# Attention outputs of the neighbourhood heads stored by block, tables loaded a block earlier, and result rows in five buffers that are first read six steps behind their load

## The chip, the cores and the metric

The kernel runs on one core of a Trainium2 chip. The metric is the device time of one execution in microseconds (us). Names of engines are those of the profile: PE (TensorE matmuls), PEld (its weight loads), DVE (VectorE), ACT (ScalarE), POOL (GpSimd), SP (SyncE, which here only issues DMAs; SPq is its queue in the trace).

## The reference

Two layers of a transformer over 2048 latent tokens (a grid of 32 rows by 64 columns) and 256 context tokens, width 1024, all in float32. Cut to what matters here, one layer is:

```
q, k, v, ... = split(h @ w_in)                       # three groups of heads
mix_a = windowed attention with sink, 6 heads        # 384 columns
mix_b = gated short convolution                      # 256 columns
mix_c = neighbourhood attention, 6 heads             # 384 columns
        s = q . k / 8 + rel_pos_bias[dr, dc]         # window of 8 grid rows x 16 columns, and all context keys
x = layer_norm(alpha * x + gate1 * (concat(mix_a, mix_b, mix_c) @ w_out))
route each of 16 experts to its 256 best tokens      # expert choice
acc = alpha * x + sum over experts of gate * swiglu(x[chosen]) at the chosen rows
x = layer_norm(acc)                                  # after layer 1: the output, 2048 x 1024
```

In layer 1 only the latent tokens are computed past the projections.

## The kernel before

Each layer l runs four phases one after another: phase_in (projections), phase_att, phase_out (output projection, first layer norm) and phase_moe (routing is between the two). float32 matmuls are done as three matmuls on a high part (cast by ACT) and a low part (subtracted by DVE). Instructions of an engine and the DMAs of a queue run in the order in which the program emits them. The waits between engines are put in by the framework that the kernel is written with; SP's DMAs share eight completion lanes (DMAHW0 to 7) in rotation, so that each also waits for the one eight before it on its lane.

**Attention.** phase_att works through two A units (the windowed heads) and then six C units, one for each neighbourhood head. A C unit has blocks n = 0 to 3, each a group of 16 grid columns with all 32 rows; in layer 0 a block 4 of context tokens comes first. A block has four steps m of 128 queries; in each, PE makes logits `lg` (L1088, L1089), DVE adds a bias table and takes the maximum (L1113, a custom instruction that also moves the logits), ACT exponentiates (L1121), PE transposes the probabilities (L1139, L1162), ACT and DVE make their high and low parts `ph`, `pl` (L1267, L1258), and PE multiplies with the values (L1197). At a block's end the result is transposed back (L1215), divided by the sums (reciprocal L1226, multiplication L1234) and stored to the DRAM tensor MIXC. A group of blocks shares one tile `o`: reciprocal, multiplication and store come at a group's last block. Groups are the blocks (4), (0, 1), (2, 3), and in the last unit (4), (0, 1), (2), (3). A store is issued in four pieces a block (L1246), by SP, but by POOL for the last block of all.

The bias tables of a unit (`bias` and `va`, 128 x 2048) are made by POOL (bias_part, L1052: three instructions a table) from a tile `toep`, which SP loads in load_unit behind the unit's k (two DMAs of 64 x 2304) and context values vx. load_unit for the next unit is called at block 1 of the present one; before it in each block, more_queries and more_values load q and vw some blocks ahead.

**Output projection.** phase_out loads for each tile of 128 tokens `mix` (384 columns from MIXA, 384 from MIXC), transposes these on PE (L1352), splits them on ACT and DVE (L1354, L1356) and multiplies with w_out (L1369), whose high and low parts are made by ACT and DVE on the way (L178, L186). Ahead of the first tile SP issues the loads of two tiles and of some row vectors (`row`, L1318). The scratch of phase_att and phase_out lie over each other in SBUF, by the order in which the pools are opened.

**Experts and the last layer norm.** phase_moe runs 16 experts. T and F are lists of generators that a tick advances; a tick follows each group of matmuls, 16 an expert. In layer 1, experts 13 to 15 (FINK = 3) run beside the final layer norm of the result's rows: fin_early takes a buffer `fx` (3 of them) or an unused one (`xe`, fin_next), loads 128 rows of ACC (L1841, SP), and adds fin_tile, which waits FINGO = 2 ticks, sums the rows on ACT (L1866), squares them (L1872), scales them on DVE (L1887, L1891) and stores them (L1882). The rows that the last three experts chose are gathered, normalised and scattered once more behind them (L1829, L1850). Expert outputs `y` (DVE, L1765) are added to ACC by POOL's scatters (L1784) from four buffers.

Of the kernel before, what the change touches and what calls it, by code (L numbers as in the profile page):

```python
# [7 lines left out]
F32 = mybir.dt.float32  # L8
# [57 lines left out]
FINLAG = 4  # L66
FINGO = 2
FINSTEP = 4
# [156 lines left out]
def build(ctx, tc, t, out):  # L225
# [47 lines left out]
    def dr(name, shape, dt=F32):  # L273
        return [dram.tile(shape, dt, name=f"{name}{i}") for i in range(DEPTH)]
# [8 lines left out]
    MIXA = dr("MIXA", [TT, 384])  # L283
    MIXC = dr("MIXC", [TT, 384])
    MODR = dr("MODR", [2, 48 * 128])
# [615 lines left out]
    def phase_att(l):  # L901
# [15 lines left out]
        hp.append(pool("at_h1"))  # L917
        lp.append(pool("at_w1"))
        shift(es, 64)
        kp.append(pool("at_k1"))  # L920
        op = pool("at_o", 3)
        bsp = pool("at_bias")
# [16 lines left out]

        units, blks, st = {}, {}, {}  # L940
        blist, mem = [], []
# [10 lines left out]
        for kind, u in [("A", 0), ("A", 1)] + [("C", u) for u in range(6)]:  # L952
            for rows in (range(2, 6), range(6, 10), range(10, 14), range(14, NT), (0, 1)) if kind == "A" else (
                    ((4,), (0, 1), (2,), (3,)) if u == 5 else ((4,), (0, 1), (2, 3))):
                for j, n in enumerate(rows):
                    group[kind, u, n] = ((kind, u, rows[0]), j, len(rows))
# [8 lines left out]
        def load_unit(kind, u):  # L965
# [17 lines left out]
            if kind == "C":  # L983
                v = vxp.tile([128, 2, 128], F32R, name="vx")
                SY.dma_start(v.bitcast(F32), vs[:, 0:2, 2 + u, :])
                r["v"] = v

                tz = tp.tile([128, 16, 64], F32, name="toep")
                rp = t["rpb"][l, u]
                n = 15 * 64 + 48  # L990
                SY.dma_start(tz.rearrange("p i j -> p (i j)")[:, 0:n],
                             bass.AP(tensor=rp.tensor, offset=rp.offset + 15, ap=[[64, 8], [-1, 16], [1, n]]))
                r["toep"] = tz

# [41 lines left out]
        def bias_part(u, ct, rt):  # L1036
# [8 lines left out]
            if rt == 0:  # L1045
                r["bias", ct] = biases[ct % 2 if u % 2 == 0 else 1 - ct % 2]
            b, tz = r["bias", ct], r["toep"]
            j0 = (16, 8, 0)[ct]
# [8 lines left out]
        def qk(i):  # L1057
            b, m, nm = mem[i]
            kind, u, n = b
            if m == 0:  # L1060
# [8 lines left out]
                if at == ustart[kind, u] + (4 if kind == "A" else 1) and x < len(ulist):  # L1069
                    load_unit(*ulist[x])  # L1070
                if (kind, u) == ("C", 5) and at == ustart[kind, u] + 1:
                    W.open(6, 8)
# [94 lines left out]
        def pv(b, nm):  # L1167
# [72 lines left out]
            elif n == 4:  # L1240
                SY.dma_start(MIXC[l][0:256, 64 * u:64 * u + 64].rearrange("(m p) d -> p m d", p=128), all_)
            else:
                dst = MIXC[l][256:TT, 64 * u:64 * u + 64].rearrange("(m a g b) d -> m g a b d", m=4, a=8, g=4)
                for x in range(ng):
                    for m in range(4):
                        (G if b == blist[-1] else SY).dma_start(dst[m, n0 + x], all_[:, 4 * x + m, :])  # L1246
            del st["of", g]
# [55 lines left out]
    def phase_out(l, aff):  # L1303
# [34 lines left out]
        def load_c(n):  # L1338
            SY.dma_start(loaded[n][0][:, 384:768], MIXC[l][tiles[n] * 128:tiles[n] * 128 + 128, :])

# [235 lines left out]
    def phase_moe(l, aff):  # L1576
# [182 lines left out]
        def put(e, n, a, j, py, ys, gates):  # L1759
            yield STEP  # L1760
            if j == 0:
                ys[a] = sb.tile([128, D], F32, name="y", bufs=4)
            y = ys[a][:n, 512 * j:512 * j + 512]
# [41 lines left out]
        def fin_next():  # L1805

            while True:
                for name, n in (("fx", 3), ("xe0", 2), ("xe1", 2)):
                    got = used.setdefault(name, [])
# [50 lines left out]
        def fin_tile(n):  # L1860

            m = fp.tile([128, 6], F32, name="fm", bufs=10)
            sq = junk[:, 0:D]
            for _ in range(FINGO):
                yield STEP
# [212 lines left out]
```

## Time and profile before

| | |
|---|---|
| median of 3 runs | 4123.91 us (4122.41 to 4124.77) |
| the profiled execution | 4118.89 us, its span 4117.1 us |
| busy share of the span | PE 92%, DVE 70%, ACT 49%, POOL 18% |
| mean granted TensorE clock | 0.957 of full speed |
| C units of layer 0 | 808 to 1056 us |
| phase_out of layer 0, first matmul | 1067.80 us |
| C units of layer 1 | 2895 to 3126 us |
| phase_out of layer 1, first matmul | 3136.82 us |
| experts 13 to 15 of layer 1, with the final norm | 3936 to 4067 us |
| what is left behind the last expert | 4067 to 4117 us |

The execution that the profiler recorded took 5.0 us less than the median of the unprofiled runs; the span is that of the trace within it. An engine's busy time is the union of its instructions, so a share below 100% on PE is time in which PE waited.

### The profile page before, as it was taken

What the parts mean: (1) busy time and instruction counts of PE and PEld (TensorE: products, weight loads), DVE (VectorE), ACT (ScalarE), POOL (GpSimd) and SP (SyncE); (2) the same over time, 40 slices, a digit from 0 to 9 for tenths busy, and PEclk for the clock granted to TensorE, in tenths of its full rate; (3) what the DMA queues carried; (4) which work ended last, traced back from release to release, by engine and by line L of the source; (5) the groups of instructions that cost most, each with busy time, mean ns of one, the idle gap of its engine ahead of it and who ended that gap; (6) DMA issues with size and microseconds to landing.
All of it is one profiled execution on the core that took longest, in us unless ns stands there. A gap on an engine that the chain in (4) does not pass through costs nothing. (4 is left out here: it accounts for less than half of the span.)

```text
span 4117.1 us, 63491 instructions
## 1 busy us (share of the span) xinstructions
PE 3801.6 (92%) x23004; PEld 3249.1 (79%) x23004; DVE 2869.1 (70%) x5588; ACT 2010.3 (49%) x3884; POOL 726.0 (18%) x680
## 2 busy tenths in 40 slices
PE   7999999998898899999996999999988976999983
PEld 5887888887787378998984888889887865999972
DVE  6555559987677467777756766479876777777765
ACT  4344339987433144444433534369875333444453
POOL 0000000122133023232211100000321221221214
PEclk9999999999999899999998999999999987999996
DMA  7566674578743677777756765573887424888885
GB/s 238 167 209 192 202 207 129 111 148 154 231 158 126 191 238 227 221 214 209 214 169 218 236 200 183 175 194 88 148 156 209 172 107 156 246 253 257 245 241 185
DMA packets 763969, 784.68 MB, mean 191 GB/s; under 512 B 140224, under 2 KB 645800, under 8 KB 761608
## 3 DMA queue, kind: packets, MB, share of 16 engines
q1 hardware_dynamic: 727800, 656.44, 54.7%
q0 software_dynamic: 34704, 123.13, 10.8%
q8 instruction: 182, 2.98, 0.3%
q10 hardware_dynamic: 1152, 1.05, 0.1%
q14 instruction: 131, 1.07, 0.1%
HBM read 601.98 MB, written 178.48 MB: 190 GB/s over the span
## 5 line engine op out<-in xcount | busy, mean ns | idle before, releaser
L178 ACT CAST wh<-wraw 128x1024 fp32r<-128x1024 f32 x636 | 657.2, 1051 | 394.1 <-DMA wraw<-in_w_in 121.8
L186 DVE TENSOR_TENSOR wl<-wraw,wh 128x1024 fp32r<-128x1024 f32 x636 | 751.5, 1216 | 40.9 <-ACT wh L178 40.7
L1258 DVE TENSOR_TENSOR pl<-pt,ph 128x256 fp32r<-128x256 f32 (+2 forms) x792 | 361.0, 496 | 27.0 <-ACT ph L1267 12.4
L635 PE MATMUL gem<-hh,wh 128*128 128x512 f32 (+1 forms) x960 | 352.9, 368 | 0.0
L1267 ACT CAST ph<-pt 128x256 fp32r<-128x256 f32 (+2 forms) x792 | 310.2, 447 | 86.7 <-PE pt L1139 69.6
L1121 ACT ACTIVATE p<-lg,mx 128x640 f32<-128x640 f32 (+3 forms) x408 | 332.2, 814 | 40.0 <-DVE mx L1113 38.4
L637 PE MATMUL gem<-hh,wl 128*128 128x512 f32 (+1 forms) x960 | 348.6, 363 | 0.0
L636 PE MATMUL gem<-hl,wh 128*128 128x512 f32 (+1 forms) x960 | 347.0, 361 | 0.0
L1922 PE MATMUL pu<-xh,wh 128*128 128x288 f32 (+1 forms) x1024 | 303.1, 296 | 9.2 <-DVE sa L1750 9.2
L1922 PE MATMUL pa<-xh,wh 128*128 128x288 f32 (+1 forms) x1024 | 299.7, 293 | 0.0
L1088 PE MATMUL lg<-k,q 128*128 128x384 f32 (+2 forms) x768 | 282.0, 389 | 17.7 <-ACT p L1121 8.9
L1923 PE MATMUL pa<-xl,wh 128*128 128x288 f32 (+1 forms) x1024 | 295.7, 289 | 0.0
L1924 PE MATMUL pa<-xh,wl 128*128 128x288 f32 (+1 forms) x1024 | 295.7, 289 | 0.0
L1924 PE MATMUL pu<-xh,wl 128*128 128x288 f32 (+1 forms) x1024 | 295.4, 288 | 0.0
L1923 PE MATMUL pu<-xl,wh 128*128 128x288 f32 (+1 forms) x1024 | 295.0, 288 | 0.0
L1642 POOL DMA_INDIRECT xe<-H,ix x80 | 161.1, 2014 | 469.0 <-DVE ix L1637 349.5
L1089 PE MATMUL lg<-k,q 128*128 128x256 f32 x816 | 228.1, 286 | 0.3 <-DVE pl L1258 0.3
L1784 POOL DMA_INDIRECT ACC<-y,ix x62 | 123.3, 1989 | 583.3 <-DVE y L1765 323.2
L1959 PE MATMUL py<-wh,gh 128*128 128x512 f32 x512 | 206.3, 403 | 18.4 <-ACT gh L1752 9.9
L810 PE MATMUL gem<-wh,hh 128*128 128x512 f32 x544 | 219.3, 403 | 1.0 <-ACT hh L603 1.0
L811 PE MATMUL gem<-wl,hh 128*128 128x512 f32 x544 | 215.6, 396 | 1.4 <-DVE wl L186 1.4
L812 PE MATMUL gem<-wh,hl 128*128 128x512 f32 x544 | 215.5, 396 | 0.0
(367 smaller groups left out, 9659.5 us busy)
## 6 DMA issues: line engine op xcount, KB each, us to landing
wraw<-in_w_in SPq DMA_DIRECT2D x160, 512.0 KB
wraw<-in_w_gate SPq DMA_DIRECT2D x128, 512.0 KB
wraw<-in_w_up SPq DMA_DIRECT2D x128, 512.0 KB
wraw<-in_w_down SPq DMA_DIRECT2D x128, 512.0 KB
wraw<-in_w_mod SPq DMA_DIRECT2D x88, 512.0 KB
vw<-VS SPq DMA_DIRECT2D x192, 128.0 KB
q<-QA SPq DMA_DIRECT2D x204, 96.0 KB
VS<-vs SPq DMA_DIRECT2D x36, 512.0 KB
```

Of the source, the lines that this page charges most:

```text
L178: self.nc.scalar.copy(h, self.raw[i])
L186: self.nc.vector.tensor_tensor(e[1], self.raw[i], e[0].bitcast(F32), op=ALU.subtract)
L635: P.matmul(pg[:, t0:nt], wh[:, cs_], hh[:, k, t0:nt], start=(k == 0), stop=False)
L636: P.matmul(pg[:, t0:nt], wh[:, cs_], hl[:, k, t0:nt], start=False, stop=False)
L637: P.matmul(pg[:, t0:nt], wl[:, cs_], hh[:, k, t0:nt], start=False, stop=(k == KD - 1))
L1088: P.matmul(pl[:, w0:512], q[:, x, m, :], win(k), start=(x == 0), stop=(x == 1))
L1121: S.activation(p[:, 0:768 - w0], rec["lg"][:, w0:768], AF.Exp, bias=st[b]["mx"][:, m:m + 1], scale=-1.0, accum_out=st[b]["ss"][:, m:m + 1])
L1258: V.tensor_tensor(view(st[b]["pl"]), src, view(st[b]["ph"].bitcast(F32)), op=ALU.subtract)
L1267: S.copy(view(st[b]["ph"]), src)
L1922: P.matmul(pp[f], wh[:, cs_], xh[:, kk, :], start=(kk == 0), stop=False)
L1923: P.matmul(pp[f], wh[:, cs_], xl[:, kk, :], start=False, stop=False)
L1924: P.matmul(pp[f], wl[:, cs_], xh[:, kk, :], start=False, stop=(kk == KD - 1))
```

## The change

Five things are changed.

1. The rows of the neighbourhood heads lie in a tensor MIXC (context, unchanged form) and a new MIXL [4, 128, 4, 384] (block, partition, m, column), which has the form of the tile `o`: a block's store is one DMA of 128 partitions x 4 x 64 instead of four. Each block is a group of its own, so reciprocal and multiplication come once a block.
2. load_c reads the 128 latent rows of a tile from MIXL by two DMAs of 64 partitions.
3. The pool at_o (tile `o`) is opened ahead of shift() and at_k1, two pools of the same size changing places.
4. `toep` is loaded by a function of its own, in the iteration of the first block of the unit before instead of its second, where k and vx are still loaded.
5. FINGO is 6 (1 once the last expert is through), `fx` has five buffers, and `y` two in the last layer.

```diff
--- before.py
+++ after.py
@@ -64,7 +64,7 @@
 
 FINK = 3
 FINLAG = 4
-FINGO = 2
+FINGO = 6
 FINSTEP = 4
 FINSTEP2 = 2
 
@@ -281,7 +281,9 @@
     VS = dr("VS", [TT, 8, 128])
     OB = dr("OB", [2, 128, 2, TT])
     MIXA = dr("MIXA", [TT, 384])
-    MIXC = dr("MIXC", [TT, 384])
+
+    MIXC = dr("MIXC", [CTX, 384])
+    MIXL = dr("MIXL", [4, 128, 4, 384])
     MODR = dr("MODR", [2, 48 * 128])
     H2 = [dram.tile([n, HX], F32, name=f"H2{n}") for n in (TT, SEQ)]
     ACC = dr("ACC", [SEQ, D])
@@ -916,9 +918,9 @@
         lp = [pool("at_w0")]
         hp.append(pool("at_h1"))
         lp.append(pool("at_w1"))
+        op = pool("at_o", 3)
         shift(es, 64)
         kp.append(pool("at_k1"))
-        op = pool("at_o", 3)
         bsp = pool("at_bias")
         tp = pool("at_toep", 2)
         vwp = pool("at_vw", 3)
@@ -937,7 +939,7 @@
         biases = [None, bsp.tile([128, BWID], F32, name="bias")]
         sink = sinks[:, l, :]
 
-        units, blks, st = {}, {}, {}
+        units, blks, st, toeps = {}, {}, {}, {}
         blist, mem = [], []
         for u in range(2):
             blist += [("A", u, n) for n in range(2, NT)] + ([] if last else [("A", u, 0), ("A", u, 1)])
@@ -951,7 +953,7 @@
         group = {}
         for kind, u in [("A", 0), ("A", 1)] + [("C", u) for u in range(6)]:
             for rows in (range(2, 6), range(6, 10), range(10, 14), range(14, NT), (0, 1)) if kind == "A" else (
-                    ((4,), (0, 1), (2,), (3,)) if u == 5 else ((4,), (0, 1), (2, 3))):
+                    [(n,) for n in range(5)]):
                 for j, n in enumerate(rows):
                     group[kind, u, n] = ((kind, u, rows[0]), j, len(rows))
         ulist = [("A", u) for u in range(2)] + [("C", u) for u in range(6)]
@@ -985,12 +987,14 @@
                 SY.dma_start(v.bitcast(F32), vs[:, 0:2, 2 + u, :])
                 r["v"] = v
 
-                tz = tp.tile([128, 16, 64], F32, name="toep")
-                rp = t["rpb"][l, u]
-                n = 15 * 64 + 48
-                SY.dma_start(tz.rearrange("p i j -> p (i j)")[:, 0:n],
-                             bass.AP(tensor=rp.tensor, offset=rp.offset + 15, ap=[[64, 8], [-1, 16], [1, n]]))
-                r["toep"] = tz
+        def load_toep(u):
+
+            tz = tp.tile([128, 16, 64], F32, name="toep")
+            rp = t["rpb"][l, u]
+            n = 15 * 64 + 48
+            SY.dma_start(tz.rearrange("p i j -> p (i j)")[:, 0:n],
+                         bass.AP(tensor=rp.tensor, offset=rp.offset + 15, ap=[[64, 8], [-1, 16], [1, n]]))
+            toeps[u] = tz
 
         def load_queries(at):
             b = blist[at]
@@ -1044,7 +1048,7 @@
                     G.memset(biases[0][:, o:o + 256], 0.0)
             if rt == 0:
                 r["bias", ct] = biases[ct % 2 if u % 2 == 0 else 1 - ct % 2]
-            b, tz = r["bias", ct], r["toep"]
+            b, tz = r["bias", ct], toeps[u]
             j0 = (16, 8, 0)[ct]
             i0, n = ((4, 12), (0, 16), (0, 12))[rt]
             o = BOFF[rt]
@@ -1068,6 +1072,8 @@
                 more_values(at + 3)
                 if at == ustart[kind, u] + (4 if kind == "A" else 1) and x < len(ulist):
                     load_unit(*ulist[x])
+                if at == ustart[kind, u] and x < len(ulist) and ulist[x][0] == "C":
+                    load_toep(ulist[x][1])
                 if (kind, u) == ("C", 5) and at == ustart[kind, u] + 1:
                     W.open(6, 8)
             k = units[kind, u]["k"]
@@ -1238,12 +1244,9 @@
                 SY.dma_start(MIXA[l][128 * n0:128 * (n0 + ng), 192 * u:192 * u + 192].rearrange("(b p) c -> p b c", p=128),
                              all_.rearrange("p (b m) d -> p b (m d)", b=ng))
             elif n == 4:
-                SY.dma_start(MIXC[l][0:256, 64 * u:64 * u + 64].rearrange("(m p) d -> p m d", p=128), all_)
+                SY.dma_start(MIXC[l][:, 64 * u:64 * u + 64].rearrange("(m p) d -> p m d", p=128), all_)
             else:
-                dst = MIXC[l][256:TT, 64 * u:64 * u + 64].rearrange("(m a g b) d -> m g a b d", m=4, a=8, g=4)
-                for x in range(ng):
-                    for m in range(4):
-                        (G if b == blist[-1] else SY).dma_start(dst[m, n0 + x], all_[:, 4 * x + m, :])
+                (G if b == blist[-1] else SY).dma_start(MIXL[l][n][:, :, 64 * u:64 * u + 64], all_)
             del st["of", g]
 
         gens = []
@@ -1336,7 +1339,13 @@
                 load_c(n)
 
         def load_c(n):
-            SY.dma_start(loaded[n][0][:, 384:768], MIXC[l][tiles[n] * 128:tiles[n] * 128 + 128, :])
+            m, i = loaded[n][0], tiles[n]
+            if i < 2:
+                SY.dma_start(m[:, 384:768], MIXC[l][i * 128:i * 128 + 128, :])
+                return
+            src = MIXL[l].rearrange("g (a b) m c -> m a g b c", b=16)[(i - 2) // 4]
+            for r in range(2):
+                SY.dma_start(m[64 * r:64 * r + 64, 384:768], src[2 * ((i - 2) % 4) + r])
 
         def load_x(n):
             if n >= len(tiles):
@@ -1759,7 +1768,7 @@
         def put(e, n, a, j, py, ys, gates):
             yield STEP
             if j == 0:
-                ys[a] = sb.tile([128, D], F32, name="y", bufs=4)
+                ys[a] = sb.tile([128, D], F32, name="y", bufs=2 if last else 4)
             y = ys[a][:n, 512 * j:512 * j + 512]
             if a < 2:
                 V.scalar_tensor_tensor(y, py, gates[:, a:a + 1], g2[:, 512 * j:512 * j + 512], op0=ALU.mult, op1=ALU.mult)
@@ -1805,7 +1814,7 @@
         def fin_next():
 
             while True:
-                for name, n in (("fx", 3), ("xe0", 2), ("xe1", 2)):
+                for name, n in (("fx", 5), ("xe0", 2), ("xe1", 2)):
                     got = used.setdefault(name, [])
                     q = len(got)
                     if name == "fx":
@@ -1861,7 +1870,8 @@
 
             m = fp.tile([128, 6], F32, name="fm", bufs=10)
             sq = junk[:, 0:D]
-            for _ in range(FINGO):
+
+            for _ in range(1 if "end" in flags else FINGO):
                 yield STEP
             S.activation(sq, xs[n], AF.Copy, accum_out=m[:, 5:6])
             yield STEP
```

On SP's queue in the C units of layer 1, before (the stretch that holds one toep load; q and vw are queries and values, k and vx those of the next unit, MIXC<-o the stores):

```order
1001 L1009 DMA q_26948<-QC_85 64x8x64 x3
1002 L1021 DMA vw<-VS_89 32x8x128 x4
1003 L978 DMA k<-KC_87 64x2304 x2
1004 L985 DMA vx<-VS_89 128x2x128
1005 L991 DMA toep<-in_rpb 128x1x1008
1006 L1009 DMA q_26949<-QC_85 64x8x64 x3
1007 L1021 DMA vw<-VS_89 32x8x128 x4
1008 L1246 DMA MIXC_95<-o 8x16x64 x8
1009 L1009 DMA q_26950<-QC_85 64x8x64 x3
```

The same engine and unit in the changed kernel:

```order
1012 L1025 DMA vw<-VS_89 32x8x128 x4
1013 L995 DMA toep<-in_rpb 128x1x1008
1014 L1249 DMA MIXL_97<-o 512x1x64
1015 L1013 DMA q_26960<-QC_85 64x8x64 x3
1016 L1025 DMA vw<-VS_89 32x8x128 x4
1017 L980 DMA k<-KC_87 64x2304 x2
1018 L987 DMA vx<-VS_89 128x2x128
1019 L1249 DMA MIXL_97<-o 512x1x64
1020 L1013 DMA q_26961<-QC_85 64x8x64 x3
```

toep stands ahead of a block's q and vw and of k and vx, where it stood behind them, and eight stores on two blocks have become two, one a block.

On SP's queue at the end of attention in layer 0 and at the start of phase_out, before, with what each DMA waits for (the four rows ahead of these are stores as well; `m` is a row vector, POOL's DMAs are on lanes DMASW):

```order
803 L1246 DMA MIXC_94<-o 8x16x64 [waits DMAHW0_49,DVE_49]
804 L1246 DMA MIXC_94<-o 8x16x64 [waits DMAHW1_49]
805 L1246 DMA MIXC_94<-o 8x16x64 [waits DMAHW2_49]
806 L1246 DMA MIXC_94<-o 8x16x64 [waits DMAHW3_49]
807 L1329 DMA mix<-MIXA_92 128x384 [waits DMAHW4_49]
808 L1333 DMA mh<-OB_90 128x2x128 [waits DMAHW5_49]
809 L1333 DMA ml<-OB_90 128x2x128 [waits DMAHW6_49]
810 L1329 DMA mix<-MIXA_92 128x384 [waits DMAHW7_49]
811 L1333 DMA mh<-OB_90 128x2x128 [waits DMAHW0_49]
812 L1333 DMA ml<-OB_90 128x2x128 [waits DMAHW1_49]
813 L1318 DMA m_11795<-MODR_96 128x1024 [waits DMAHW2_49,PE_49,Activation_49]
814 L1345 DMA xr<-in_ctx 128x1024 [waits DMAHW3_49,DVE_49]
```

The same place in the changed kernel:

```order
735 L1249 DMA MIXL_96<-o 512x1x64 [waits DMAHW4_49,DVE_49]
736 L1249 DMA MIXL_96<-o 512x1x64 [waits DMAHW5_49,DVE_49]
737 L1249 DMA MIXL_96<-o 512x1x64 [waits DMAHW6_49,DVE_49]
738 L1332 DMA mix<-MIXA_92 128x384 [waits DMAHW7_49]
739 L1336 DMA mh<-OB_90 128x2x128 [waits DMAHW0_49]
740 L1336 DMA ml<-OB_90 128x2x128 [waits DMAHW1_49]
741 L1332 DMA mix<-MIXA_92 128x384 [waits DMAHW2_49]
742 L1336 DMA mh<-OB_90 128x2x128 [waits DMAHW3_49]
743 L1336 DMA ml<-OB_90 128x2x128 [waits DMAHW4_49]
744 L1321 DMA m_11791<-MODR_98 128x1024 [waits DMAHW5_49,DMASW5_49,DMAHW6_49,DVE_49,Activation_49]
745 L1354 DMA xr<-in_ctx 128x1024
```

Three stores stand ahead of the first `mix` load instead of twelve; and the row vector `m` now waits for POOL's store (DMASW5) and for the last of SP's. On ACT, the first cast of w_out in phase_out (the first L178 behind the last L1221) waited for all of POOL's stores and the eight lanes of SP, and waits in the changed kernel for loads of attention, ACT and POOL's instructions, but for no store:

```order
1147 L1221 COPY o_11676<-pt_11670 128x256 [waits DMAHW4_49,DMAHW3_49,DMAHW5_49,DMAHW2_49,DMAHW6_49,DMAHW1_49,DMAHW7_49,DMAHW0_49,PE_49]
1148 L1203 COPY ot_11708<-po_11681 128x512 [waits PE_49]
1149 L1221 COPY o_11715<-pt_11710 128x256 [waits DMAHW7_49,PE_49]
1150 L178 CAST wh_11806<-wraw_11150 128x1024 [waits DMAHW1_49,DMAHW0_49,DMAHW2_49,DMASW7_49,DMAHW3_49,DMASW6_49,DMAHW4_49,DMASW5_49,DMAHW5_49,DMASW0_49,DMAHW6_49,DVE_49,DMAHW7_49,Activation_49,Pool_49]
1151 L178 CAST wh_11809<-wraw_11152 128x1024
1152 L1354 CAST mh_11785<-pt_11815 128x384 [waits PE_49]
1153 L1354 CAST mh_11791<-pt_11820 128x384 [waits PE_49]
```

In the changed kernel:

```order
1147 L1227 COPY o_11678<-pt_11672 128x256 [waits DMAHW3_49,PE_49]
1148 L1209 COPY ot_11707<-po_11683 128x512 [waits PE_49]
1149 L1227 COPY o_11714<-pt_11709 128x256 [waits DMAHW4_49,PE_49]
1150 L178 CAST wh_11802<-wraw_11155 128x1024 [waits DMAHW1_49,DMAHW6_49,DMAHW0_49,DMAHW7_49,Activation_49,Pool_49]
1151 L178 CAST wh_11805<-wraw_11157 128x1024
1152 L1363 CAST mh_11781<-pt_11811 128x384 [waits PE_49]
1153 L1363 CAST mh_11787<-pt_11816 128x384 [waits PE_49]
```

The cast has lost the four lanes DMASW.

On ACT beside expert 13 in layer 1, before, where the first row tile is touched (L178 casts expert weights; L1745 and L1752 belong to an expert's gate):

```order
2694 L178 CAST wh<-wraw 128x1024 x2
2695 L1745 ACTIVATE sa<-pa 128x256 x2
2696 L1866 ACTIVATE junkb,fm<-fx 128x1024
2697 L178 CAST wh<-wraw 128x1024
2698 L1752 CAST gh<-sa 128x256
2699 L1872 ACTIVATE junkb,fm<-fx,fm 128x1024
2700 L1752 CAST gh<-sa 128x256
2701 L1866 ACTIVATE junkb,fm<-fx 128x1024
2702 L1872 ACTIVATE junkb,fm<-fx,fm 128x1024
```

The same place in the changed kernel:

```order
2694 L178 CAST wh<-wraw 128x1024 x2
2695 L1754 ACTIVATE sa<-pa 128x256 x2
2696 L178 CAST wh<-wraw 128x1024
2697 L1761 CAST gh<-sa 128x256 x2
2698 L1876 ACTIVATE junkb,fm<-fx 128x1024
2699 L1882 ACTIVATE junkb,fm<-fx,fm 128x1024
2700 L178 CAST wh<-wraw 128x1024 x2
2701 L1876 ACTIVATE junkb,fm<-fx 128x1024
2702 L178 CAST wh<-wraw 128x1024 x4
```

The first sum over a row tile (L1866, in the changed kernel L1876) comes behind the gate casts L1752 (L1761) of its part of the expert, where it came ahead of them.

## Rows read from the trace of the kernel before

**Rows 1.** Stage windows: length, busy PE, PEld, DVE, ACT, POOL; clock, DMA share, GB/s.

```profile
...
808.00:1056.00 248.00, 227.10 (x1593) 198.72 (x1593) 206.86 (x500) 194.08 (x493) 58.82 (x53) 0.97 0.81 156
2895.00:3126.00 231.00, 213.01 (x1507) 192.25 (x1505) 189.81 (x441) 180.80 (x440) 52.55 (x49) 0.96 0.82 153
3142.00:3385.00 243.00, 228.33 (x1263) 185.75 (x1261) 170.73 (x298) 89.35 (x146) 67.34 (x96) 0.96 0.45 159
3487.00:3917.00 430.00, 428.13 (x3075) 399.96 (x3074) 320.30 (x433) 202.94 (x288) 90.45 (x49) 1.00 0.84 251
3917.00:4067.00 150.00, 117.73 (x759) 106.34 (x758) 100.22 (x147) 74.12 (x118) 32.96 (x36) 0.90 0.75 228
...
```

**Rows 2.** Waits of DVE, C units of layer 1 (us in total, times, longest).

```profile
...
DVE lg L1113 <- POOL bias L1052: 13.4, 4, 6.1
...
DVE lg L1113 <- POOL va L1052: 8.7, 2, 5.0
...
```

**Rows 3.** Timeline of one stall in these units, SP (start us, us, instruction).

```profile
...
2993.26 0.66 SPq L991 DMA_DIRECT2D toep<-in_rpb  x1
...
```

**Rows 4.** Timeline of the same stall, POOL.

```profile
...
3006.11 2.22 POOL L1052 TENSOR_TENSOR bias<-maskC,toep 128x384 f32<-128x384 f32 x2 [30.12 <-DMA toep<-in_rpb]
```

**Rows 5.** Timeline of the same stall, DVE.

```profile
...
2990.56 0.83 DVE L1113 CUSTOM_DVE_ANT_0 lg<-lg,bias 128x640 f32<-128x640 f32 x1 [0.17 <-PE lg L1089]
...
3007.14 0.83 DVE L1113 CUSTOM_DVE_ANT_0 lg<-lg,bias 128x640 f32<-128x640 f32 x1 [6.06 <-POOL bias L1052]
...
```

**Rows 6.** Waits of PE, C units of layer 0.

```profile
...
PE lg L1088 <- DMA q<-QC: 7.2, 4, 3.8
...
```

**Rows 7.** Timeline, end of attention and start of phase_out, layer 0.

```profile
...
1055.13 0.46 SPq L1329 DMA_DIRECT2D mix<-MIXA  x1
...
1057.05 2.49 POOL L1246 DMA_DIRECT2D MIXC<-o  x4 [33.44 <-DVE o L1234]
...
1060.07 0.90 PE L1352 MATMUL pt<-ident,mix 128*128 128x128 f32 x3 [1.42 <-DMA mh<-OB]
...
1065.34 1.99 ACT L178 CAST wh<-wraw 128x1024 fp32r<-128x1024 f32 x2 [9.50 <-DMA xr<-in_ctx]
...
1067.80 0.77 PE L1369 MATMUL po<-wh,mh 128*128 128x512 f32 x1 [6.83 <-ACT mh L1354]
...
```

**Rows 8.** Timeline of the same place in layer 1, all engines.

```profile
...
3125.78 0.37 ACT L1221 COPY o<-pt 128x256 f32<-128x256 f32 x1 [0.75 <-PE pt L1215]
...
3132.01 0.90 PE L1352 MATMUL pt<-ident,mix 128*128 128x128 f32 x3 [1.67 <-DMA mix<-MIXA]
...
3136.82 1.19 PE L1369 MATMUL po<-wh,mh 128*128 128x512 f32 x2 [3.91 <-DMA xr<-X]
...
```

**Rows 9.** Waits of ACT beside the last three experts.

```profile
...
ACT junkb L1866 <- DMA fx<-ACC: 43.1, 8, 9.8
...
```

**Rows 10.** Waits of PE beside the last three experts.

```profile
...
PE py L1959 <- ACT gh L1752: 9.9, 2, 7.0
PE pu L1922 <- DVE sa L1750: 9.2, 2, 5.0
PE py L1959 <- DVE y L1765: 6.4, 2, 4.2
...
```

**Rows 11.** Groups of ACT instructions by form, 3917 us to the end.

```profile
...
L1872 ACT ACTIVATE junkb<-fx,fm 128x1024 bf16<-128x1024 f32 x14 | 16.1, 1150 | 7.4 <-DVE fm L1870 6.5 <-DVE fm L1868 0.8
L1866 ACT ACTIVATE junkb<-fx 128x1024 bf16<-128x1024 f32 x14 | 14.8, 1058 | 43.5 <-DMA fx<-ACC 43.1
...
```

**Rows 12.** Groups of DVE instructions by form, C units of layer 1.

```profile
...
L1234 DVE TENSOR_TENSOR o<-o,rs 128x512 f32<-128x512 f32 x11 | 7.5, 683 | 0.0
...
L1234 DVE TENSOR_TENSOR o<-o,rs 128x256 f32<-128x256 f32 x1 | 0.4, 425 | 0.0
L1226 DVE RECIPROCAL rs<-ss 128x4 f32<-128x4 f32 x2 | 0.3, 168 | 0.0
...
```

**Rows 13.** Scatters of y, experts of layer 1.

```profile
...
DMA to landing us min/median/max: 6.3/9.8/11.0
```

## Prediction

> **What bounds the kernel now.** The page gives PE 92% of the span, so only places where PE stands still can pay much, and one table by stage finds them [rows 1]: PE is busy 227.1 of 248 us in the C units of layer 0, 213.0 of 231 in those of layer 1, and 117.7 of 150 from expert 13 to the end of the last one, which leaves 20.9, 18.0 and 32.3 us. The change also touches the two passages from attention to phase_out, which I read row by row, and what follows the last expert, where PE does nothing.
>
> In the C units of layer 1 the list of waits says why: DVE stood 13.4 and 8.7 us, 22.1 in six stalls, before L1113 for tables of POOL [rows 2]. One stall: SP issues toep at 2993.26 [rows 3], POOL begins at 3006.11 after 30.12 us of waiting for it [rows 4], and DVE goes on at 3007.14 after 6.06 us [rows 5]. So toep needs 12.9 us from issue to use, behind k and vx. In layer 0 DVE does not wait so; PE waits 7.2 us for queries [rows 6], which SP issues behind toep and behind eight stores.
>
> At the end of attention in layer 0, PE has transposed the second tile of phase_out at 1060.97 (1060.07 + 0.90), but ACT casts w_out only from 1065.34, after 9.50 us of idling, and the first matmul comes at 1067.80 [rows 7]. The wait is put down to a load, yet the order shows the cast waiting for POOL's four stores as well. The last of these is issued by 1059.54 (1057.05 + 2.49), 5.8 us ahead of the cast, a landing time near the 6.3 us that is the least of POOL's scatters [rows 13]. I take the stores as the releaser. Layer 1 reads alike, with transposes through at 3132.91 and the first matmul at 3136.82 [rows 8].
>
> Beside the last experts, ACT waits 43.1 us in eight waits for rows of ACC [rows 9]. ACT runs in order, so the casts and gates of the expert queue up behind, and PE waits 9.9, 9.2 and 6.4 us for them [rows 10]: 25.5 of its 32.3 us.
>
> **The change, part by part.**
>
> *Early toep.* In the shown stall DVE is through with the old table at 2991.4 (2990.56 + 0.83), so POOL may overwrite from there. toep is issued a block earlier, 9.6 us (231 us for 24 blocks): 2983.7, and even if it takes the same 12.9 us without k and vx ahead of it, POOL begins at 2996.6 and its first instruction ends at 2997.7 (two take 2.22). DVE asks for it at 3001.1 (3007.14 − 6.06). The 6.06 us fall away, and so do the other five stalls, none longer. DVE's 22.1 us are not all PE's: PE has 18.0 to give, and some stays for other reasons. I take −16, between −8 (only the stalls of the first table go) and −22. What is late next is PE itself.
>
> *Queries in layer 0.* toep no longer stands ahead of them, and one store a block stands there instead of eight on two: −7 of 7.2 (between −2, if the transfers themselves are late, and −10).
>
> *One group a block.* Two scalings of 425 ns replace one of 683, with one more reciprocal of 168 [rows 12]: 0.335 us a pair, 22 pairs in two layers, 7.4 us of DVE. DVE has 41 us free in each stage (248 − 206.9, 231 − 189.8 [rows 1]), but is in the chain of each step: +3, between 0 and +7.4.
>
> *Fewer stores, at_o moved.* The cast of w_out no longer waits for stores. In layer 0 ACT is free at 1055.84 (1065.34 − 9.50), and its two casts end at 1057.8. The first mix load, issued at 1055.13, stands behind four stores of the block that DVE scaled last for SP, and then behind one: at 0.62 us a store (2.49 for four) it moves up by 1.9, and the transposes with it, from 1060.97 to 1059.1. First matmul near 1059.3: −8.5. In layer 1 ACT is free at 3126.15 (3125.78 + 0.37), casts until 3128.15, and half a microsecond for the split gives a matmul near 3128.8: −8. Together −16.5. If the mix loads don't move, the transposes hold it, with 0.4 for the split: 1061.4 and 3133.4, −6.4 and −3.4, −9.8 in all. At the other end the granted clock, which falls while PE stands, falls less: 2 us more in each layer, −20.5. SP now waits at the row vector m for POOL's store, and xr, the C halves of mix, lg, lb and two parts of w_out are behind it. That store is one of 0.62 us, not four: issued by 1057.7, it should have landed by 1063.5 if it too takes 5.8. The C halves are first wanted behind five eighths of the product of two tiles, some 19 us of PE at 243 us for 16 tiles [rows 1]. If that cover were gone, the few us by which SP goes on later would be PE's. I count nothing.
>
> *load_c in two DMAs.* SP issues 32 more, about half a microsecond each (0.46 for a mix load in [rows 7]), and has little else there. A C half is loaded a tile ahead, and a tile takes 15.2 us (243 for 16). Nothing. [...] No run here shows the engines of one DMA.
>
> *The final norm.* Four more ticks, each a sixteenth of an expert of 35.8 us (430 for 12 of them [rows 1]), are 9.0 us; the longest wait of ACT for a row tile is 9.8 and the mean 5.4 [rows 9]. Nearly all end before ACT comes to them. Five buffers cover the longer hold. PE gets back most of its 32.3 us; the rest stays with DVE, which has a tile's work to put between an expert's. That is −22 (between −12, half the named waits, and −28). Tiles touched later end later. The order has eight tiles touched behind the last product, not six; a tile costs ACT 1.06 + 1.15 us [rows 11], some 2.6 with the short reads behind each, so +5.2 by ACT, and ACT has idle time there that takes some: +3 (0 to +8). Net −19. The two `y` buffers cost nothing as long as a scatter has landed, in 6.3 to 11.0 us [rows 13], before its buffer's turn comes in the next expert, a good half of 35.8 us later.
>
> Sum: −16 − 7 + 3 − 16.5 − 19 = −55.5. The profiled execution, 4118.89, becomes 4063.4; from the median, 4123.9, it is **4068.4**. The cuts are made in the profiled one, and its 5 us below the median are taken as the same in both kernels.
>
> **Rivals.**
>
> *The norm's gain is given back.* ACT no longer waits, but the same 20 tiles of ACT and DVE work lie in three experts; DVE, 100 us busy in 150 already [rows 1], becomes their bound, and two tiles run alone at the end. Loop −12, tail +8: 15 us less, 4083. For it: DVE's load; against it: a third of DVE's time there is idle.
>
> *The tables are not what is late.* The transfers are: DMA is busy 0.81 and 0.82 of the C stages [rows 1]. toep comes earlier, k, q and vw then later, and of −16 and −7 remain −8 and −2: 4081. Against it: toep is a fixed amount, and it moves out of the crowd with k. With the rival above: 4096.
>
> *Slower: the two half loads.* If a half of 64 rows uses only a few of the engines, four say, it lands later. Phase_out takes 159 GB/s at a share of 0.45 [rows 1], or 22 GB/s for each of 16 engines when busy. A C half of 197 KB over four of them is 2.2 us, 4.1 with the other traffic, against 0.6 over sixteen. The cover is 15.2 us. [...] Only from a landing 1.7 us past it would 32 tiles lose 55 us and the kernel come out slower, at 4124 and up.
>
> *It doesn't do what it says.* The waits change their names only: toep meets the same backlog, the norm is bound by its scatters, and the passages give their least, −9.8, against DVE's +7.4. 4121.5, not to be told from before.
>
> **How the numbers follow.** The forecast has 0.58 (its own range 4050 to 4078), the norm's rival 0.15, the tables' 0.12, both 0.05, the loads 0.04, no effect 0.06. With every cost at its low end the sum falls by 6, 3, 3, 4 and 9 us to 4043, so little lies under 4046; with every one at its high end it rises by 8, 5, 4.4, 6.7 and 15 us to 4107, and 4100 takes in both rivals together. 0.2%, or 8.2 us, is about what a measurement can tell here. Faster by more than that: 0.58 + 0.15 + 0.12 + 0.05 = 0.90; within: 0.06; slower: 0.04.
>
> **What would show it.** Right: no wait of L1113 for POOL above 1 us in layer 1; first matmuls of phase_out 8 us sooner after the last block; ACT's waits for fx under 10 us in all, PE busy nine tenths of the last three experts, and a tail of 50 to 55 us. Wrong: POOL's tables still beginning 13 us behind k, PE waiting for k or q instead, ACT's cast waiting for a load behind SP's stop at m, transposes waiting for MIXL, DVE without gaps beside experts 13 to 15, or a tail of 60 us.

## The result

The changed kernel takes 4078.66 us (median of 4, 4077.98 to 4079.84) against 4123.16 beside it: a ratio of 0.9894 (95% interval 0.9877 to 0.9912), 44.5 us less where 55.5 were forecast. The profiled executions differ by 40.9 us, span 4076.2 against 4117.1. From the starts of the first and last matmuls of each stage (transposes of outputs, L1215 and now L1221; po, L1369 and L1378; first expert matmul and py; of the three products of a po or py the first):

| stretch | before, us | after, us | difference | forecast |
|---|---|---|---|---|
| attention, layer 0 (first to last transpose of outputs) | 424.0 | 411.9 | −12.1 | −5.5 |
| its end to the last po, layer 0 | 262.0 | 252.8 | −9.2 | −8.5 |
| attention, layer 1 | 395.2 | 388.1 | −7.1 | −14.5 |
| its end to the last po, layer 1 | 232.2 | 230.2 | −2.0 | −8 |
| experts of layer 1, first matmul to last py | 611.4 | 595.4 | −16.0 | −22 |
| last py to the end | 57.0 | 62.1 | +5.1 | +3 |

What lies between adds 0.4. (The forecast's +3 for DVE is split over the two attentions.) Stage windows of the changed kernel, C units of both layers, phase_out of layer 1, and the last experts (columns as in [rows 1]):

```profile
808.00:1043.00 235.00, 221.80 (x1590) 194.60 (x1588) 212.23 (x521) 192.62 (x491) 58.27 (x53) 0.99 0.79 165
2870.00:3098.00 228.00, 213.53 (x1530) 191.82 (x1528) 200.64 (x471) 182.95 (x450) 57.06 (x52) 0.98 0.79 160
3112.00:3355.00 243.00, 224.02 (x1237) 182.04 (x1236) 169.71 (x296) 89.56 (x146) 68.30 (x97) 0.95 0.47 165
3886.00:4020.00 134.00, 113.39 (x762) 103.48 (x760) 94.04 (x139) 69.24 (x110) 29.37 (x32) 0.93 0.79 239
```

In layer 1 PE still stands 14.5 us in its C units. From the list of waits of all engines there, changed kernel:

```profile
...
DVE o L1234 <- ACT o L1227: 18.3, 6, 3.9
ACT o L1227 <- DMA MIXL<-o: 16.8, 5, 4.2
...
PE lg L1094 <- ACT p L1127: 12.5, 5, 3.4
...
DVE lg L1119 <- PE lg L1095: 3.7, 6, 1.0
```

DVE's waits for tables [rows 2] have shrunk to one of 0.7 us. In their place ACT waits 16.8 us before it writes an output tile `o`, for the store that still reads the tile's last content, and PE 12.5 us behind ACT. One such wait in the timeline of the changed kernel:

```profile
2910.72 1.06 DVE L1240 TENSOR_TENSOR o<-o,rs 128x256 f32<-128x256 f32 x1
...
2924.80 1.28 SPq L980 DMA_DIRECT2D k<-KC  x2
...
2926.81 0.56 SPq L1249 DMA_DIRECT2D MIXL<-o  x1
...
2936.44 0.37 ACT L1227 COPY o<-pt 128x256 f32<-128x256 f32 x1 [3.33 <-DMA MIXL<-o]
```

The block scaled at 2910.72 is stored by SP only at 2926.81, behind the next unit's k, and the store has landed and the tile is free at 2936.4, 26 us after the scaling. (SP issues the stores in the order of the blocks; that of the block scaled next, at 2919.07, is issued at 2937.22.) There are three tiles; a tile held two blocks before and holds one now, so it is wanted again after three blocks, not six.

The passage in layer 0 came out as forecast (answers to [rows 7]):

```profile
1042.46 0.37 ACT L1227 COPY o<-pt 128x256 f32<-128x256 f32 x1 [0.74 <-PE pt L1221]
1042.73 1.99 ACT L178 CAST wh<-wraw 128x1024 fp32r<-128x1024 f32 x2
...
1044.04 0.78 POOL L1249 DMA_DIRECT2D MIXL<-o  x1 [33.02 <-DVE o L1240]
...
1045.47 0.90 PE L1361 MATMUL pt<-ident,mix 128*128 128x128 f32 x3 [1.85 <-DMA mix<-MIXA]
...
1046.03 1.20 PE L1378 MATMUL po<-wh,mh 128*128 128x512 f32 x2
```

ACT casts w_out straight behind its last output, ahead of POOL's store, and the first po comes 3.6 us behind the end of the last transposes; 12.4 before. In layer 1 that passage is as short, but phase_out itself is 5.7 us longer (226.6 us from first to last po, 220.9 before):

```profile
3098.57 0.76 POOL L1249 DMA_DIRECT2D MIXL<-o  x1 [36.38 <-DVE o L1240]
...
3106.49 2.36 SPq L1348 DMA_DIRECT2D mix<-MIXL  x4
...
3115.56 4.16 SPq L1332 DMA_DIRECT2D mix<-MIXA  x1
...
3120.76 2.12 SPq L1348 DMA_DIRECT2D mix<-MIXL  x2
...
3128.81 0.52 PE L1361 MATMUL pt<-ident,mix 128*128 128x128 f32 x3 [3.95 <-DMA mix<-MIXL]
```

SP stands until 3106.49 for POOL's store, 7.9 us after its issue, and PE waits 3.95 us for the third tile.

Beside the last experts, the waits of the changed kernel answer to [rows 9, 10]:

```profile
ACT wh L178 <- DMA wraw<-in_w_down: 26.3, 3, 15.6
...
PE py L1969 <- ACT gh L1761: 11.6, 2, 6.0
...
PE pu L1932 <- DVE sa L1759: 3.5, 1, 3.5
ACT junkb L1876 <- DMA fx<-ACC: 3.3, 2, 2.5
```

ACT's 43.1 us for row tiles are 3.3, but it now waits 26.3 us for w_down, and the waits in PE's list still come to 15.6 us, where those of [rows 10] come to 25.5.

### The profile page after: what moved, and what is told of

The parts are those of the page before. It is cut to its first block, busy times and chain, and to the rows that moved or that the text cites. A ratio compares the mean times of both kernels' runs of the same rounds, so it can differ in the third digit from the quotient of the medians.

```text
span 4076.2 us, 63337 instructions
## 1 busy us (share of the span) xinstructions
PE 3789.0 (93%) x23004; PEld 3239.2 (79%) x23004; DVE 2882.1 (71%) x5632; ACT 2005.9 (49%) x3884; POOL 721.6 (18%) x674
## 5 line engine op out<-in xcount | busy, mean ns | idle before, releaser
L178 ACT CAST wh<-wraw 128x1024 fp32r<-128x1024 f32 x636 | 656.3, 1049 | 401.2 <-DMA wraw<-in_w_in 121.2
```

The costliest lines, as they stand in the source:

```text
L178: self.nc.scalar.copy(h, self.raw[i])
```

## The experiments

Ratios are to the kernel before, on the same chip; compare them with 0.9894 (0.9877 to 0.9912). Times are medians of four to six executions; beside them the kernel before takes 4119.1 to 4123.9 us, so times of different runs compare to some 5 us. Traces vary as well: attention of layer 1 takes 387.6 to 392.7 us in the changed kernel and in those that leave its C units alone, and the expert loop (first expert matmul of layer 1 to the last py) 594.3 to 598.4 us in those that leave the norm alone. The end is what follows the last py.

**The norm undone.**

```diff
-FINGO = 6
+FINGO = 2
-... name="y", bufs=2 if last else 4)
+... name="y", bufs=4)
-for name, n in (("fx", 5), ...
+for name, n in (("fx", 3), ...
-for _ in range(1 if "end" in flags else FINGO):
+for _ in range(FINGO):
```

> The changed kernel with the fifth part undone: FINGO 2, three fx buffers, four y buffers. Theory, from the two traces (the loop shorter by 15.5 us, the end longer by 5.1): 10 us slower, 4089. By the prediction's term of 19: 4098.

Measured 4088.23, 0.9915 (0.9901 to 0.9929). The loop is 610.8 us, the end 56.7: by the traces the norm's part is worth 15.4 − 5.4 = 10 us, as expected, and not 19. The medians say the same (9.6 us), but the intervals of the two ratios overlap.

**toep late.**

```diff
-                if at == ustart[kind, u] and ... ulist[x][0] == "C":
-                    load_toep(ulist[x][1])
                     load_unit(*ulist[x])
+                    if ulist[x][0] == "C":
+                        load_toep(ulist[x][1])
```

> The changed kernel with toep loaded behind the next unit's k and vx again. By the prediction's terms (16 in layer 1, some of 7 in layer 0): 4095 to 4102. Rival: the waits for tables and those for stores stand at the same unit boundaries and hide each other, so that only some 6 us come back: 4085.

Measured 4094.34, 0.9929 (0.9915 to 0.9942): some 15 us slower. All of it is layer 1 (406.7 us against 388.1); in layer 0 attention takes 410.0 against 411.9, so there toep's place is worth nothing. But the time is not lost where the prediction said. Waits in the C units of layer 1 of this kernel:

```profile
ACT o L1227 <- DMA MIXL<-o: 29.6, 5, 7.0
...
PE lg L1094 <- ACT p L1127: 25.9, 6, 6.2
...
DVE lg L1119 <- POOL bias L1056: 2.4, 1, 2.4
```

DVE waits 2.4 us for a table; ACT waits 29.6 for stores, which SP now issues behind toep too.

**More output tiles**, first in a pool of their own, opened behind at_q.

```diff
+        ocp = pool("at_oc")
 ...
-                of["o"] = op.tile([128, 12, 64], F32, name="o")[:, 0:ng * nm, :]
+                if kind == "A":
+                    of["o"] = op.tile([128, 12, 64], F32, name="o")[:, 0:ng * nm, :]
+                else:
+                    of["o"] = ocp.tile([128, 4, 64], F32, name="oc", bufs=6)[:, 0:ng * nm, :]
```

> The changed kernel, with six tiles of its own for the outputs of neighbourhood blocks in place of three shared with the windowed heads. Theory: in layer 1 ACT stands 16.8 us for stores that still hold an output tile, and PE 12.5 us behind it; with three more blocks of slack that goes, the C units of layer 1 end 10 to 12 us sooner, and the time is near 4067. Rival: DVE, 200.6 us busy in 228, is what holds these units, and the waits only change their name: 4075 to 4079.

Measured 4072.62, 0.9878 (0.9863 to 0.9893). Attention of layer 1 is 369.1 us, 19.0 less, more than the theory asked; but the passages to phase_out grew from 3.9 and 3.6 us to 9.8 and 9.7 (last transpose to first po), since SP's first mix load now stands for stores (6.1 us in layer 1), and each layer began its attention some 5 us later. So three blocks share one of the old tiles, with nothing else moved:

```diff
+        third = [0, None]
 ...
+                    x = third[0] % 3
+                    if x == 0:
+                        third[1] = op.tile([128, 12, 64], F32, name="o")
+                    of["o"] = third[1][:, 4 * x:4 * x + nm, :]
+                    third[0] += 1
```

> The changed kernel, where three neighbourhood blocks take a third each of one output tile, so that the three tiles hold nine blocks and nothing else in memory moves. Theory: in layer 1 the stores that hold output tiles cost the C units what the kernel with six tiles of its own saved between the same transposes (19 us there); with the memory unmoved nothing of it is given back at the ends of attention: 4060. Rival: the saving of that kernel came from its other places in memory; then 4072 to 4078.

Measured 4053.93, 0.9827 (0.9811 to 0.9844), 66 us under the kernel before. Attention of layer 1 is 368.8 us, that of layer 0 406.2. Its C units, both layers:

```profile
808.00:1038.00 230.00, 220.68 (x1593) 193.80 (x1593) 212.34 (x522) 192.97 (x492) 58.26 (x53) 1.00 0.83 169
2867.00:3075.00 208.00, 206.20 (x1524) 186.92 (x1523) 198.70 (x469) 182.12 (x448) 56.62 (x52) 1.00 0.87 174
```

In layer 1 PE stands 1.8 of 208 us. That settles the new wait: too few output tiles, not DVE, cost these units some 19 us.

**toep late, with the tiles by thirds.**

> Output tiles by thirds, and toep behind k and vx as before. In the changed kernel the late toep cost 15 us, but there ACT waited for stores (29.6 us) and not DVE for tables (2.4). Theory: with the stores out of the way DVE's waits for tables come back (22 us before), nearly all in layer 1: 4070 to 4074 beside 4054 with the early toep. Rival: what the late toep cost was the stores' landing behind it; then nothing holds DVE here and the time is 4054 to 4058.

Measured 4059.76, 0.9855 (0.9838 to 0.9873): 6 us more than by thirds with the early toep by the medians, 12 by the ratios, whose intervals overlap. DVE's waits in the C units of layer 1 are back in part:

```profile
DVE lg L1120 <- POOL bias L1057: 6.9, 4, 2.7
DVE lg L1120 <- POOL va L1057: 4.2, 2, 2.6
```

11.1 us where the kernel before had 22.1, at the same place of toep: both expectations were off. Attention of layer 1 takes 377.6 us, 17.6 less than before with toep late in both. So the block stores, a group a block and enough tiles together gave about as much there as all that was forecast for toep; toep's place gave 8.8, and some 4 of it are given back behind attention (from the last transposes to the last po 226.3 us with the late toep, 230.3 with the early one).

**at_o unmoved.**

> The changed kernel with at_o back behind shift and at_k1. By the prediction the passages to phase_out gain 16.5 us by the move and the fewer stores together. If the move carries it (the cast waits for the last store again): some 5 to 8 us come back, because one store of POOL lands sooner than four: 4084 to 4087. If the fewer stores carry it: within 2 us, 4078 to 4081.

Measured 4092.16, 0.9927 (0.9912 to 0.9942), some 13 us slower, more than either case. The end of attention in layer 0 of this kernel:

```profile
1043.69 0.37 ACT L1227 COPY o<-pt 128x256 f32<-128x256 f32 x1 [0.74 <-PE pt L1221]
...
1045.28 0.78 POOL L1249 DMA_DIRECT2D MIXL<-o  x1 [33.03 <-DVE o L1240]
...
1052.30 1.99 ACT L178 CAST wh<-wraw 128x1024 fp32r<-128x1024 f32 x2 [8.24 <-DMA xr<-in_ctx]
1054.77 1.20 PE L1378 MATMUL po<-wh,mh 128*128 128x512 f32 x2 [7.77 <-ACT mh L1363]
```

The cast is put down to xr, as before, and comes 7.0 us behind the issue of POOL's one store, where it came 8.3 behind the first of four [rows 7]. From last transpose to first po it is 11.4 and 11.5 us, against 12.6 and 11.3 before: the move carries the passages, the fewer stores next to nothing. Which wait is the long one can be read from the instructions that wait ahead of the cast, one or two semaphores each: here the last long one ends at 1052.11, and the semaphore of POOL's store reaches its full count at 1052.08; before, they were 1065.14 and 1065.12. So the cast does wait for POOL's last store. In layer 1 the move buys little, though: phase_out of this kernel takes 221.0 us from first to last po, as before, where the changed kernel takes 226.6. SP stands at the C loads there just as long (3111.28 to 3118.23), but PE, which starts 7.9 us later, waits for no C half.

**The last store in four, and the C loads later.** Two kernels on the 5.7 us of phase_out in layer 1.

```diff
+                    for m in range(4):
+                        G.dma_start(MIXL[l][n][:, m, 64 * u:64 * u + 64], all_[:, m, :])
```

> The changed kernel, with the last block's store (POOL) in four DMAs, one a quarter m, as before. Theory: in layer 1 SP stands 7.5 us at the first load from MIXL for the whole of that store to land (7.9 us), and phase_out loses 5.7 us behind it; the first tile needs one quarter alone, so SP goes on 3 to 4 us sooner and the time is 4075 (4 us less). Rival: the loads of 64 rows are slow by themselves, on few engines: no change, 4078 to 4079.

Measured 4076.47, 0.9886 (0.9871 to 0.9901); SP goes on at 3110.28, still 6.4 us after the first quarter's issue at 3103.92. PE waits 3.3 us for the third tile, and first to last po takes 224.7 us.

```diff
-        load_c(0)
-        load_c(1)
         for k in range(5):
+            if k == 2:
+                load_c(0)
+                load_c(1)
```

> The changed kernel, where phase_out issues the first two tiles' loads from MIXL behind two parts of the product, not ahead of lg, lb and the parts of w_out. Theory: SP no longer stands 7.5 us at them in layer 1 with the row vectors, w_out and the third tile's loads behind it; PE's 4.0 us at the third tile go, and the time is 4074 (4 to 5 us less). Rival: the transfers themselves are late (DMA at 0.98 and 299 GB/s there), or the loads of 64 rows are slow: 4078 to 4079.

Measured 4082.19, 0.9902 (0.9884 to 0.9919). PE waits 4.1 us for C halves; 224.3 us. Neither is told apart from the changed kernel by time. Each gets back some 2 of the 5.7 us by the trace, so SP's stop is at most a part. With at_o unmoved the 5.7 us were not lost, with the same loads, the same store and the same stop: 4.0 of them are the third tile's load, met sooner by a PE that starts sooner. Why that load is no earlier stays open.

**Sixteen rows a load**, on the tiles by thirds, from the third tile on.

```diff
+                for g in range(4):
+                    p = 64 * r + 16 * g
+                    SY.dma_start(m[p:p + 16, 384:768], src[2 * ((i - 2) % 4) + r][g])
```

> Output tiles by thirds, and the C half of the third tile and those behind it loaded by eight DMAs of 16 rows, not two of 64. PE stands 3.6 us for the third tile in layer 1; its C half is through SP at 3099.8 and transposed at 3105.2, 5.4 us later. If two DMAs on few engines are what is late: that gap falls to 2 to 3 us, and PE's wait with it by 1 to 2 us. If the crowd on the DMA engines is: the gap stays, and six more issues of 0.5 us make PE wait longer, 5 to 7 us in layer 1. In both cases the time is within 4 us of 4054.

Measured 4052.12, 0.9833 (0.9820 to 0.9847), the same as by thirds. The third tile's C half, from the first issue to its transposes, takes 7.1 us (3090.60 to 3097.66) against 7.6 (3097.66 to 3105.22); from the last issue 1.8 against 5.4. The issues themselves take 5.25 us instead of 2.14, so time and waits do not tell few engines from a crowd. The counts of the DMAs' completion semaphores, each of which the trace holds, differ: all 64 half loads of the changed kernel are counted five times, once within 0.6 us of the end of the issue and four times as the data lands, where each load of 128 rows before was counted 16 times and each load of 16 rows is too; what one count stands for no run shows. The two half loads of the third tile by thirds land 5.8 and 6.9 us after their issue, the eight small ones 2.0 to 4.7 us after theirs, and yet the last of them lands 6.6 us after the first issue, against 7.4. In time nothing shows.

**The norm's loads on POOL's queue.**

```diff
-                    SY.dma_start(xs[n], ACC[1][128 * n:128 * n + 128, :])
+                    G.dma_start(xs[n], ACC[1][128 * n:128 * n + 128, :])
```

> The changed kernel, with the row tiles of the final norm loaded by POOL's queue instead of SP's. Theory: what the norm still costs beside the last experts is SP, which stands 35.8 us for scatters and 25.4 for buffers at these loads, with w_down behind it (ACT waits 26.3 us for it): without them on SP, ACT's wait for w_down falls under 8 us and the loop is 6 to 10 us shorter, 4070. Rival: POOL now stands at the loads, with the norm's roots and the scatters of y behind it: 4080 to 4090.

Measured 4080.94, 0.9901 (0.9883 to 0.9918); the loop is 595.4 us, as in the changed kernel. Waits beside its last experts:

```profile
ACT gh L1761 <- DVE sa L1759: 33.5, 7, 11.5
DVE fx L1901 <- POOL fm L507: 21.9, 4, 9.6
...
ACT wh L178 <- DMA wraw<-in_w_down: 2.2, 1, 2.2
```

ACT's wait for w_down went from 26.3 to 2.2 us, as the theory asked, and DVE's wait for POOL's roots took its place (21.9 against 7.9), as the rival did. PE's waits come to 15.6 us, as in the changed kernel. SP's stop is real, and its cure on this queue costs the same.

**The delay**, on the tiles by thirds, with `FINGO = 2` and `FINGO = 4`.

> Output tiles by thirds, with FINGO 2 and the five fx buffers kept. If the delay is what frees ACT: its waits for fx come back, 20 us and more of 43, the loop is 8 to 12 us longer, the end 3 to 5 us shorter: 4058 to 4063. If the two more buffers are: 4050 to 4053, the loop kept and the end shorter.

Measured 4061.88, 0.9858 (0.9843 to 0.9873). The loop is 606.7 us against 598.4, the end 57.4 against 62.6. ACT's waits for row tiles, 3.1 us by thirds, are back:

```profile
ACT junkb L1884 <- DMA fx<-ACC: 36.6, 7, 8.8
```

So it is the delay that frees ACT, not the two buffers.

> Output tiles by thirds, with FINGO 4: one tile less is left behind the last product (6, not 7, behind the second statistic). If two ticks (4.5 us) cover most of ACT's waits: the loop within 3 us, the end 2.6 us shorter, 4051 to 4055. If not: 4056 to 4060.

Measured 4052.93, 0.9835 (0.9822 to 0.9849): loop 600.6, end 58.4. ACT waits 10.6 us for row tiles. The loop keeps most of its gain and 4.2 us less lie at the end; the time can't be told from FINGO 6. Of the loop's 15.4 us, the delay gave 8 to 12 (606.7 to between 598.4 and 594.3); the buffers' 4 (610.8 to 606.7) are no more than loops vary by.

## Why the prediction was right, and where it was not

The time lies in the stated range of 4046 to 4100, 0.7 us above the forecast's own, and the largest waits named were the ones that went. That the sum came as near as it did is in part luck: by the table the parts miss by up to 7.4 us, layer 0 ahead of the forecast, layer 1 and the experts behind it. The 5 us by which the profiled execution lies under its median were taken as the same in both kernels; in the changed one they are 0.6, which is why 40.9 us by the traces are 44.5 by the medians. Undone one at a time, the norm, toep's place and the move of at_o come to some 10, 15 and 13 us; the block stores and the group a block were undone in no run. By its steps:

- **Early toep (−16) and one group a block (+3, 0 to +7.4).** The waits for tables went as said. The second step failed: it priced DVE's added instructions and left out that a group is also the life of an output tile. The price was too low as well, 425 ns from the one block whose scaling it could see: 30 of the 47 new scalings took 987 to 1180 ns, each while POOL made a table, and 17 took 403 to 426, none of them beside POOL. With the reciprocals DVE's part rose by some 23 us, not 7.4, most of it hidden, since with enough tiles PE stands 1.8 us. Three tiles for three blocks put 16.8 us of waiting on ACT; the tiles by thirds get 19.3 us back. Without that wait, attention of layer 1 would have gained 26.4 us (395.2 to 368.8; 23 of it in the windows of the C units), more than the 18.0 at which the prediction capped it: PE's busy time, which the cap took as fixed, fell as well, from 213.0 to 206.2 us, with the granted clock at 1.00 instead of 0.96.
- **How much is toep's.** In the changed kernel its place is worth about 15 us, near the −16, but mostly by letting stores land sooner (ACT waits 16.8 us for them, and 29.6 with the late toep); with enough tiles it is 8.8 us of attention, some 4 of them given back behind it, and the time does not tell the two kernels apart. What the prediction put on toep went in good part with the fewer stores; that these had crowded SP's queue ahead of toep is my reading, which no run takes apart.
- **Queries in layer 0 (−7).** −12.1 came, none of it from toep's place. The wait went as said: no wait for q is left in PE's list for the C units of layer 0, and PE stands 13.2 us in their window where it stood 20.9. What the term left out is PE's busy time, 221.8 us there against 227.1, at a granted clock of 0.99 against 0.97.
- **The passages (−16.5).** The passages lost 8.7 and 7.7 us, and nearly all of that is the move's: with at_o unmoved they are 7.5 and 7.9 us longer again. The reading that ACT waits for stores and not for the load named was right. The range's 2 us a layer for the granted clock were an estimate that no run shows; in layer 0 the clock was 0.53 from 1056 to 1068 us before, where PE is busy for 2.0 of the 12, and 0.52 in the 6 us of matmuls behind, and in the changed kernel 0.50 from 1046 to 1050 us and 1.00 from 1053 to 1060. "I count nothing" for SP's stop at POOL's store held in layer 0, whose first tiles read no MIXL, and not in layer 1, where phase_out gave 5.7 of the 7.7 us back; SP's stop is shown for a part of it alone. What failed there is the cover of 19 us: it is that of the first two tiles, for whose C halves PE did not wait; it waited for the third tile's, which the prediction left out. SP waits at the C loads there, not at the row vector m.
- **load_c in two (0).** Held: the loads of sixteen rows changed nothing that can be told, and with at_o unmoved phase_out of layer 1 takes 221.0 us with the two half loads, as before with one load of 128 rows. That a half load runs on few of the engines, four in the third rival's estimate, no run shows. What the traces show are counts of completion semaphores: the data of a half load lands in four, that of a load of 128 rows in 16, that of a store before (SP's) in eight and of a block's store now in 16. The halves cost nothing that shows: a half load lands 3.4 to 9.1 us after its issue, and the cover is 15.2.
- **The norm (−22 + 3).** The mechanism was right, ACT's waits for row tiles fell from 43.1 to 3.3 us. The loop's term was too large by 6: of PE's waits 15.6 us stayed, and ACT's list is now led by weights behind SP's stops. That these are the 6 us is not shown, for with the loads on POOL's queue that wait went and the loop stayed. The rival that gives gain back at the end holds in part: two tiles more cost 5.1 us.

## What to carry to other kernels

A group that sets how often something is stored often sets how long its buffer lives as well; when it is made smaller, count the blocks that the buffers cover, from the trace's time between the last write and the landing of the store. A store at the end of a phase holds whatever is laid over its tile in the next, and the wait may be booked on a load; moving the pool was worth some 13 us here. The price of an instruction wants more than one instance, and from a stretch where the other engines do what they will do: the scaling priced at 425 ns here took up to 1180. A load behind a stop on an in-order queue waits for the stop as well: ACT's wait for w_down was 26.3 us behind SP's stops at the norm's loads, and 2.2 with those on POOL's queue. Take the waits of that queue, not its busy time.

## What the runs showed of the chip that was not expected

POOL's one store of 512 pieces of 256 bytes took 7.9 us to land at the end of layer 1 and 2.5 at the end of layer 0; its four stores of 128 before took 3.1 to 6.2 us each. What SP had just issued went with it: in layer 1 the row vector m and xr (128 x 1024) go out 0.6 and 0.1 us ahead of POOL's store, in layer 0 SP stands at m until the store has landed. In the kernel with six tiles of its own SP stands until then in both layers, and the store lands in 2.4 us in both; with at_o unmoved m and xr go ahead of it in layer 0 too, and it takes 6.8 us there.

DVE's scaling of an output block (128 x 256) took 403 to 426 ns alone and 987 to 1180 ns while POOL made a table, by the same instruction of the same kernel.

PE's granted clock in the C units of layer 1 rose from 0.96 to 1.00 when its stops fell from 18.0 to 1.8 us, and its busy time there was 6.8 us less, beside the stops.
